# A hybrid decoder layer on one core: the down-projection as seven block products, with sums of its weights made under the up-projection and sums of h kept in DRAM

## The chip, the core and the metric

The kernel runs on one core of a Trainium2 chip. Five engines work side by side, each through its own queue in order: TensorE (PE; its weight loads, PEld, run beside its matmuls), VectorE (DVE), ScalarE (ACT), GpSimd (POOL) and SyncE (SP), which here only starts transfers. ACT starts some transfers too. Tiles lie in SBUF (128 partitions), matmul results in eight PSUM banks of 128x512 float32, which only DVE and ACT read here. Tensors in DRAM are reached by DMA. The metric is the device time of one execution in microseconds (us).

## The reference

One decoder layer over 2048 rows of width 1024, all in float32. The part that matters is the second half of the layer and the final norm:

```python
h = rms_norm(x, g_mlp[l]) * (1.0 + scale_m) + shift_m
u = causal_depthwise_conv(h @ w_up[l], conv_w[l], conv_b[l])
u_gate, u_val = jnp.split(u, 2, axis=-1)
x = x + gate_m * ((jax.nn.silu(u_gate) * u_val) @ w_down[l])
return rms_norm(x, g_final)
```

h is 2048x1024, w_up 1024x5504, w_down 2752x1024. In front of it stand the adaLN vectors, one input projection, two kinds of attention (16 heads) and the output projection.

## The kernel before

**Precision.** An operand x is split into hi and lo of a reduced float32 format: ACT copies x to hi, DVE or POOL subtracts hi from x to get lo (`split`, lines 43 to 45). A product is hi\*hi + hi\*lo + lo\*hi, three matmuls.

**Order.** The program is written as Python loops; a scheduler places each instruction in its engine's queue by an estimated time, within what the buffers allow (`bufs=` is the number of copies of a tile, and a new use waits for the last reader of the old one). Queues then run strictly in order.

**Output projection.** Eight groups of 256 rows (u = 0 to 7). `out_proj` multiplies `mix` by `wo` (L629), adds x (L633) and stores x1 to `x1s`. `finish_out` norms the rows, transposes them in eight pieces on TensorE (L713), lets ACT apply scale and shift into `hf_m` (L715, two buffers), and stores them from ACT's queue to `hm`, one tensor for each of eight pieces kt of h's width and each half (1024 rows) of the rows.

**Up-projection.** For each half `sblk` of the rows and each ci of 21 column blocks, a gate block and a value block of 128 columns are made together. They are treated as a 2x2 block product (halves of the rows, halves of h's width, gate and value) by seven products in place of eight. The seven weight operands come from two loads `wuraw` (512 KB each, three buffers, L781), POOL's sums `ws` and `wuraw` (L796 to L802) and `split` (`wu`, seven buffers). The seven operands of h, `oa` and `ob`, are made once per half by `h_operands` in four steps j: load a piece `xh`, form sums on POOL and DVE, split them. `pair_first` runs the first pair with all seven banks open, j outermost, since the operands arrive by j; `pair` runs the others one product of 12 matmuls after another (L810), reading banks in between (L851 to L866). `conv_tile` and L898 to L901 make the convolution, SiLU and product and store g to DRAM. A last narrow block of 64 gate and 64 value columns ends each half.

**Down-projection.** For each tb of four blocks of 512 rows, 22 pieces k of 128 rows of w_down (the last has 64): load `wdraw` and `graw`, split both, and run 3 matmuls (L960) into each of eight banks (4 row groups t, 2 column halves n). The last four k are held back and run bank by bank, so that L983 to L993 (times gate_m, plus x1, norm, store) overlap them. w_down is loaded and split four times.

Of the kernel before, what the change touches and what calls it, by code (L numbers as in the profile page):

```python
# [1 line left out]

# [31 lines left out]
def kernel(ctx: ExitStack, tc: tile.TileContext, x, c, w_ada, b_ada, g_attn, w_in, b_fgate,  # L34
# [17 lines left out]
    hms = [[dram.tile([P, 2 * TB], F32, name=f"hm{s}_{k}") for k in range(KT)] for s in range(2)]  # L52
# [10 lines left out]
    gate_m = dram.tile([P, D], F32, name="gate_m")  # L63

# [638 lines left out]
    NU = S // HT  # L703

    def finish_out(u, xts):
        sl = slice(u % 4 * HT, (u % 4 + 1) * HT)
# [3 lines left out]
        for kt in range(KT):  # L710
# [6 lines left out]
            nc.scalar.dma_start(hms[u // 4][kt][:, sl], hf)  # L717
# [3 lines left out]

    mixes = {}
    for u in range(NU):
# [10 lines left out]
        finish_out(u, xts)  # L734
    close_pool("p2b", "p2a")
# [3 lines left out]
    NK = KT // 2  # L739
    SB = 2 * TB  # L740
# [9 lines left out]
    def h_operands(sblk, j):  # L750

        pool = ho if j == 0 else ho1
        xh = ho.tile([P, 2, SB], F32, name="xh", bufs=2)
        for i in range(2):
            nc.sync.dma_start(xh[:, i], hms[sblk][j + i * NK])
        b = pool.tile([P, 3, 2, TB], F32R, name=f"ob{j}")
        a = pool.tile([P, 4, 2, TB], F32R, name=f"oa{j}")
        tt = ho.tile([P, 2, TB], F32, name="tt", bufs=1)
        t4 = wp.tile([P, TB], F32, name="t4", tag="ws", bufs=3)
        b11, b12 = xh[:, 0, 0:TB], xh[:, 0, TB:SB]  # L760
        b21, b22 = xh[:, 1, 0:TB], xh[:, 1, TB:SB]

        def put(hi, lo, s, lo_engine=None):
            split(hi, lo, s, lo_engine or nc.vector)

        nc.gpsimd.tensor_sub(tt[:, 0], b22, b12)
        nc.gpsimd.tensor_sub(b12, b12, b11)
        nc.vector.tensor_sub(tt[:, 1], b22, b12)
        nc.vector.tensor_sub(t4, b21, tt[:, 1])
        put(b[:, 0:2, 0], b[:, 0:2, 1], tt)  # L770
        put(b[:, 2, 0], b[:, 2, 1], t4)
        put(a[:, 0, 0], a[:, 0, 1], b11)
        put(a[:, 1:3, 0], a[:, 1:3, 1], xh[:, 1].rearrange("p (a n) -> p a n", n=TB), nc.gpsimd)
        put(a[:, 3, 0], a[:, 3, 1], b12)
        return [a[:, 0], b[:, 1], a[:, 1], a[:, 3], b[:, 0], a[:, 2], b[:, 2]], a
# [32 lines left out]
    def product(b, w, o, j, first, last):  # L808
        for i, (p, q) in enumerate(((0, 0), (0, 1), (1, 0))):
            nc.tensor.matmul(b, w[:, p, j], o[:, q], start=first and i == 0, stop=last and i == 2,  # L810
                             skip_group_check=True)

    def snap():
        return up_.tile([P, TB], F32, name="snap", bufs=4)
# [6 lines left out]
    def pair_first(ws, yg, yv):  # L821
# [17 lines left out]
    def pair(ws, nxt, yg, yv):  # L839

        def run(b, s, first):
            for j in range(NK):
                product(b, ws[s], obs[j][0][s], j, first and j == 0, j == NK - 1)
# [38 lines left out]
    halo = up_.tile([P, 2 * NFULL + 1, 2], F32, name="halo")  # L882
    for sblk in range(2):
        gen = w_operands(0)
        ws = []
        for j in range(NK):
            obs[j] = h_operands(sblk, j)
            ws.extend(next(gen) for _ in range(2 if j < 3 else 1))
        for ci in range(NFULL):
            nxt = w_operands(ci + 1) if ci + 1 < NFULL else None  # L890
# [10 lines left out]
            nc.sync.dma_start(gs[ci][sblk], ug)  # L901
# [4 lines left out]
        oa = [obs[j][1] for j in range(NK)]  # L906
        for j in range(NK):
            product(a, w1, oa[j][:, 0], j, j == 0, j == NK - 1)
# [112 lines left out]
```

## Time and profile before

| what | us |
|---|---|
| three runs, median (lowest to highest) | 3140.04 (3135.02 to 3141.05) |
| the profiled execution | 3137.58 |
| its span, first to last instruction | 3135.8 |
| PE busy in the span | 2962.9 (94%) |
| DVE, ACT, POOL busy | 2142.5, 1650.2, 1281.3 |
| first and last matmul of the up-projection (L810) | 1776.2 and 2644.0 |
| first matmul of the down-projection (L960) | 2653.1 |

Times within the profile count from the start of the span. "Busy" is the time in which an engine executes; matmuls are pipelined, so a row of x44 matmuls is read by where it and the next row start. A duration of one DVE or POOL instruction includes what it waits for once begun. In lists of instructions the columns are start, duration, engine, line, operation, written tile <- read tiles, shape, count, and in brackets the idle time before and what ended it. In the table of stages each engine's busy time is followed by its count of instructions, then come the granted TensorE clock (1.00 is full), the mean busy share of the DMA engines and what they moved.

### The profile page before, as it was taken

What the parts mean: (1) busy time and instruction counts of PE and PEld (TensorE: products, weight loads), DVE (VectorE), ACT (ScalarE), POOL (GpSimd) and SP (SyncE); (2) the same over time, 40 slices, a digit from 0 to 9 for tenths busy, and PEclk for the clock granted to TensorE, in tenths of its full rate; (3) what the DMA queues carried; (4) which work ended last, traced back from release to release, by engine and by line L of the source; (5) the groups of instructions that cost most, each with busy time, mean ns of one, the idle gap of its engine ahead of it and who ended that gap; (6) DMA issues with size and microseconds to landing.
All of it is one profiled execution on the core that took longest, in us unless ns stands there. A gap on an engine that the chain in (4) does not pass through costs nothing. (4 is left out here: it accounts for less than half of the span.)

```text
span 3135.8 us, 46430 instructions
## 1 busy us (share of the span) xinstructions
PE 2962.9 (94%) x15934; PEld 2508.4 (80%) x15934; DVE 2142.5 (68%) x3334; ACT 1650.2 (53%) x3033; POOL 1281.3 (41%) x1523
## 2 busy tenths in 40 slices
PE   6889998999989999999999899999899998999998
PEld 5778787878878888888877688888678887888887
DVE  6787988888866765557832677778887776254253
ACT  5665666666656665567733444444444444333332
POOL 2564455456553343352212444444544442332321
PEclk8999999999999999999999999999999999999999
DMA  9447642556346796595456532223222223554552
GB/s 268 170 149 250 175 139 64 189 178 167 124 150 184 258 279 209 152 328 137 161 186 220 195 98 81 81 81 88 77 89 86 81 81 137 186 199 161 188 200 89
DMA packets 292940, 496.51 MB, mean 158 GB/s; under 512 B 29448, under 2 KB 177664, under 8 KB 291680
## 3 DMA queue, kind: packets, MB, share of 16 engines
q1 hardware_dynamic: 281072, 480.92, 48.0%
q10 hardware_dynamic: 11632, 12.63, 1.1%
q8 instruction: 126, 2.06, 0.3%
q14 instruction: 110, 0.90, 0.1%
HBM read 352.61 MB, written 90.51 MB: 141 GB/s over the span
## 5 line engine op out<-in xcount | busy, mean ns | idle before, releaser
L810 PE MATMUL ps_o<-oa,wu 128*128 128x512 f32 x2088 | 506.2, 393 | 18.1 <-DVE oa L45 12.0
L810 PEld LDWEIGHTS ps_o<-oa,wu 128*128 128x128 f32 x2088 | 392.4, 189 | 110.0 <-DVE oa L45 15.7
L397 PE MATMUL ps_pv<-at,V 128*128 128x256 f32 x2304 | 404.7, 294 | 36.2 <-DVE at L393 19.5
L393 DVE TENSOR_TENSOR at<-ps_pt,at 128x512 fp32r<-128x512 f32 (+1 forms) x576 | 364.0, 652 | 107.2 <-ACT at L392 104.2
L281 PE MATMUL ps_pj<-hp,w_qk 128*128 128x512 f32 x1512 | 415.2, 405 | 14.2 <-DMA hp<-hs 4.4
L392 ACT ACTIVATE at<-ps_pt 128x512 fp32r<-128x512 f32 (+1 forms) x576 | 314.4, 576 | 210.2 <-PE ps_pt L388 161.0
L420 POOL TENSOR_TENSOR a<-a,r 128x512 f32<-128x512 f32 (+3 forms) x240 | 286.8, 1196 | 309.8 <-DVE r L419 88.5
L397 PEld LDWEIGHTS ps_pv<-at,V 128*128 128x128 f32 x2304 | 334.6, 191 | 81.0 <-DVE at L393 34.5
L281 PEld LDWEIGHTS ps_pj<-hp,w_qk 128*128 128x128 f32 x1512 | 275.6, 191 | 68.7 <-DMA hp<-hs 6.9
L45 DVE TENSOR_TENSOR wd<-wdraw,wd 128x1024 fp32r<-128x1024 f32 x88 | 111.8, 1271 | 263.0 <-ACT wd L44 262.9
L45 POOL TENSOR_TENSOR g<-graw,g 128x512 fp32r<-128x512 f32 x84 | 142.3, 1696 | 326.5 <-ACT g L44 325.8
L378 PE MATMUL ps_qk<-K,Q 128*128 128x512 f32 (+2 forms) x640 | 265.7, 417 | 9.6 <-DMA K<-q 5.6
L419 DVE TENSOR_TENSOR_SCAN r<-r 128x513 f32<-128x513 f32 x192 | 258.9, 1360 | 19.4 <-ACT r L410 11.5
L960 PE MATMUL ps_o<-wd,g 128*128 128x512 f32 x1040 | 251.1, 391 | 8.7 <-ACT g L44 8.7
L810 PE MATMUL ps_t<-ob,wu 128*128 128x512 f32 x984 | 242.5, 391 | 0.3 <-ACT wu L44 0.3
L379 PE MATMUL ps_qk<-K,Q 128*128 128x512 f32 (+2 forms) x640 | 237.8, 373 | 0.0
L320 PE MATMUL ps_pj<-w_v,hp 128*128 128x256 f32 (+1 forms) x1536 | 230.8, 290 | 6.6 <-DVE q L290 2.9
L960 PEld LDWEIGHTS ps_o<-wd,g 128*128 128x128 f32 x1040 | 196.2, 189 | 50.0 <-ACT g L44 9.2
L44 ACT ACTIVATE wu<-wuraw 128x512 fp32r<-128x512 f32 x214 | 133.1, 626 | 184.2 <-PE ps_o L810 111.8
L320 PEld LDWEIGHTS ps_pj<-w_v,hp 128*128 128x128 f32 x1536 | 210.1, 193 | 16.5 <-DVE q L290 3.8
L810 PEld LDWEIGHTS ps_t<-ob,wu 128*128 128x128 f32 x984 | 185.3, 189 | 39.8 <-ACT wu L44 0.7
L44 ACT ACTIVATE wd<-wdraw 128x1024 fp32r<-128x1024 f32 x88 | 93.1, 1058 | 213.3 <-PE ps_bc L960 197.9
(218 smaller groups left out, 5834.1 us busy)
## 6 DMA issues: line engine op xcount, KB each, us to landing
hp<-hs SPq DMA_DIRECT2D x224, 512.0 KB
wuraw<-in_w_up_dram SPq DMA_DIRECT2D x84, 512.0 KB
wdraw<-in_w_down_dram SPq DMA_DIRECT2D x84, 512.0 KB
Q<-q SPq DMA_DIRECT2D x128, 256.0 KB
g<-u SPq DMA_DIRECT2D x42, 512.0 KB
graw<-g SPq DMA_DIRECT2D x84, 256.0 KB
hs<-hp SPq DMA_DIRECT2D x32, 512.0 KB
K<-q SPq DMA_DIRECT2D x128, 128.0 KB
```

The source lines that it names most:

```text
L45: (lo_engine or nc.gpsimd).tensor_sub(lo, src, f(hi))
L281: nc.tensor.matmul(acc, w[kt][:, a, n], h[:, bb], start=kt == 0 and i == 0, stop=kt == KT - 1 and i == 2)
L320: nc.tensor.matmul(av[:, t * width:(t + 1) * width], hts[kt][:, a, tok], w[1][kt][:, bb, 0:width], start=kt == 0 and m == 0, stop=kt == KT ...
L378: nc.tensor.matmul(b[:, :cw], Q[:, hl, 0, qcols], K[:, hl, :cw], start=True, stop=False)
L379: nc.tensor.matmul(b[:, :cw], Q[:, hl, 1, qcols], K[:, hl, :cw], start=False, stop=True)
L392: nc.scalar.activation(at[:, 0, lo:], b[:, lo:], AF.Copy)
L393: nc.vector.tensor_sub(at[:, 1, lo:], b[:, lo:], f(at[:, 0, lo:]))
L397: nc.tensor.matmul(o[:, 0:2 * P], V[kt // 4][:, kt % 4, hl, :], rhs, start=first and kk == 0 and w == 0, stop=last and kk == 1 and w == 1)
L419: nc.vector.tensor_tensor_scan(rev, rev, rev, 1.0, ALU.mult, ALU.bypass)
L420: (nc.vector if (ch + qi) % 4 == 0 else nc.gpsimd).tensor_mul(a[:, :need], a[:, :need], r[:, 1:need + 1])
L810: nc.tensor.matmul(b, w[:, p, j], o[:, q], start=first and i == 0, stop=last and i == 2, skip_group_check=True)
L960: nc.tensor.matmul(banks[t][n], g[:, a, t * P:(t + 1) * P], w[:, b, n * TB:(n + 1) * TB], start=k == 0 and i == 0, stop=k == NKD - 1 and i ...
```

## The change

**The down-projection** becomes the seven-product scheme as well: pairs m of 128-row pieces of w_down (11 pairs, the last padded with zeros), halves of the output columns, and pairs of 128-row groups of g. Work goes in three chunks of pairs (3, 4, 4), and in each over eight row groups tp of 256 rows: 63 or 84 matmuls per unit (now L1041). The seven weight operands `wb` (from `wbraw`, three buffers) are made once per chunk and stay; the seven operands of g, `ga`, are made for each unit from `graw`. Results are added to x1 (`xo`), which is stored to `x1s` between chunks and normed in the last.

**Sums of w_down**, times gate_m, are made on POOL under the up-projection (`down_sums`, `mix_sums`) and stored to `wds`. One step of it, or of `h_sums` for the second half, is traced behind each store of g: 16 steps with POOL work in the first half, 10 in the second.

**Operands of h** are stored by operand (`hmo`). `h_sums(0)` loads, mixes on POOL and stores the sums during the last four groups of the output projection, `h_sums(1)` under the first half. `h_operand` then loads a whole operand (1 MB) and splits it, and the opening pair runs product after product.

**Buffers:** `wu` nine for seven, `snap` three for four; the last stores of g go to ACT's queue; the first weights of the second half are made at the end of the first.

```diff
+    def mix_sums(x):
+        q11, q12, q21, q22 = x
+        nc.gpsimd.tensor_sub(q22, q22, q12)
+        nc.gpsimd.tensor_sub(q12, q12, q11)
+        nc.gpsimd.tensor_add(q11, q22, q11)
+        nc.gpsimd.tensor_sub(q21, q21, q11)
+
+    def h_sums(sblk):
+        for j in range(NK):
+            x = square_tile()
+            q = [x[:, i, n * TB:(n + 1) * TB] for i in range(2) for n in range(2)]
+            for part, o in zip(q, (0, B12, 2, 5)):
+                nc.sync.dma_start(part, hmo[sblk][o][:, j])
+            mix_sums(q)
+            for part, o in ((q[3], 4), (q[1], 3), (q[0], 1), (q[2], 6)):
+                nc.sync.dma_start(hmo[sblk][o][:, j], part)
+            yield
...
         finish_out(u, xts)
+        if u >= NU // 2:
+            next(sums)
...
+    ORDER = (1, 4, 6, 0, 3, 2, 5)
+    def h_operand(sblk, o):
+        raw = square_tile().rearrange("p a (b n) -> p (a b) n", n=TB)
+        nc.sync.dma_start(raw, hmo[sblk][o])
+        b = (ho if o in ORDER[:1] else ho1).tile([P, 2, NK, TB], F32R, name=f"ob{o}")
+        split(b[:, 0], b[:, 1], raw, nc.gpsimd if o in ORDER[-2:] else nc.vector)
+        return b
+
+    def down_sums(ms):
+        gt = ho.tile([P, D], F32, name="gt", bufs=1)
+        nc.sync.dma_start(gt, gate_m)
+        yield
+        for m in ms:
...
+            for i, rows_ in ((0, P), (1, n)):
+                row = (2 * m + i) * P
+                nc.sync.dma_start(x[0:rows_, i], w_down[row:row + rows_, :])
+                nc.gpsimd.tensor_mul(x[:, i], x[:, i], gt)
+            a1, a2, b1, b2 = (x[:, i, n * TB:(n + 1) * TB] for i in range(2) for n in range(2))
+            yield
+            for o, part in ((0, a1), (2, b1), (5, b2)):
+                nc.sync.dma_start(to[o], part)
+            mix_sums((a1, a2, b1, b2))
+            for o, part in ((4, b2), (3, a2), (1, a1), (6, b1)):
+                nc.sync.dma_start(to[o], part)
+            yield
...
-        w = wp.tile([P, 2, NK, P], F32R, name="wu", bufs=7)
+        w = wp.tile([P, 2, NK, P], F32R, name="wu", bufs=9)
...
-        for j in range(NK):
-            for s in (1, 4, 6, 0, 2, 5, 3):
-                product(banks[s], ws[s], obs[j][0][s], j, j == 0, j == NK - 1)
+        for s in ORDER:
+            for j in range(NK):
+                product(banks[s], ws[s], obs[s], j, j == 0, j == NK - 1)
...
+            stored = nc.sync.dma_start(gs[ci][sblk], ug)
+            if ci >= 3 * sblk:
+                with tc.issue_after(stored.ins):
+                    next(side, None)
...
+    def down_operand(c, o):
+        n = CHUNKS[c][1]
+        w = dw.tile([P, 2, 4, TB], F32R, name="wb", bufs=7)
+        raw = wr.tile([P, 4, TB], F32, name="wbraw", bufs=3)
+        nc.sync.dma_start(raw[:, 0:n], wds[c][o])
+        split(w[:, 0, 0:n], w[:, 1, 0:n], raw[:, 0:n], nc.gpsimd if o > 4 else nc.vector)
+        return w
+
+    def g_operands(c, tp):
...
+        nc.gpsimd.tensor_sub(s3, a11, a21)
+        nc.gpsimd.tensor_add(a21, a21, a22)
+        nc.gpsimd.tensor_sub(s2, a21, a11)
+        yield put(a11)
+        yield put(s2)
+        yield put(a12)
+        nc.gpsimd.tensor_sub(a12, a12, s2)
+        yield put(a21)
+        yield put(s3, nc.gpsimd)
+        yield put(a12, nc.gpsimd)
+        yield put(a22, nc.gpsimd)
...
+        def run(b, o, first, last):
+            for m in range(n):
+                for k, (p, q) in enumerate(((0, 0), (0, 1), (1, 0))):
+                    nc.tensor.matmul(b, ga[o][:, p, m], wbs[o][:, q, m], start=first and m == 0 and k == 0,
+                                     stop=last and m == n - 1 and k == 2, skip_group_check=True)
+            if nxt is not None:
+                later.append(next(nxt))
+            if turn:
+                wlater.append(down_operand(c + 1, o))
```

**How the queues move.** First TensorE's queue where the up-projection opens. x are rows being transposed, ob and oa operands of h, ps_o, ps_t and ps_bc the banks. Before:

```order
L713 MATMUL ps_t<-edge,x_21652 128x128
L810 MATMUL ps_o<-oa_21867,wu 128x512 x2
L713 MATMUL ps_t<-edge,x_21597 128x128
L713 MATMUL ps_t<-edge,x_21652 128x128
L810 MATMUL ps_bc<-ob_21839,wu 128x512 x2
L810 MATMUL ps_o<-oa_21867,wu 128x512 x2
```

And now (the 12 matmuls of ob_21878, the first operand, stand among the last transposes of group u = 6; all 16 transposes of group u = 7 follow in one block, which ends in the first two rows):

```order
L721 MATMUL ps_t<-edge,x_21657 128x128
L721 MATMUL ps_t<-edge,x_21712 128x128
L850 MATMUL ps_t<-ob_21883,wu 128x512
L850 MATMUL ps_bc<-ob_21888,wu 128x512
L850 MATMUL ps_t<-ob_21883,wu 128x512 x11
L850 MATMUL ps_bc<-ob_21888,wu 128x512 x11
L850 MATMUL ps_o<-ob_21893,wu 128x512 x12
```

Transposes that were strewn between products now stand in front of all products but the first.

Then POOL's queue in one pair of the steady up-projection (xh holds the side work, gt is gate_m; y and halo belong to the convolution). Before:

```order
L796 TENSOR_TENSOR ws<-wuraw 128x512
L797 TENSOR_TENSOR wuraw<-wuraw 128x512
L874 COPY halo<-y 128x2
L798 TENSOR_TENSOR ws<-wuraw 128x512
L873 MEMSET y 128x2
L802 TENSOR_TENSOR wuraw<-wuraw,ws 128x512
```

And now:

```order
L736 TENSOR_TENSOR xh<-xh 128x512
L737 TENSOR_TENSOR xh<-xh 128x512
L836 TENSOR_TENSOR ws<-wuraw 128x512
L738 TENSOR_TENSOR xh<-xh 128x512
L914 COPY halo<-y 128x2
L837 TENSOR_TENSOR wuraw<-wuraw 128x512
L739 TENSOR_TENSOR xh<-xh 128x512
L838 TENSOR_TENSOR ws<-wuraw 128x512
L913 MEMSET y 128x2
L842 TENSOR_TENSOR wuraw<-wuraw,ws 128x512
```

POOL's four sums for the next weights now alternate with four sums of the side work; in every other pair two `L807 TENSOR_TENSOR xh<-xh,gt 128x1024` stand there instead.

Last, SP's queue over the same stretch. Before:

```order
L901 DMA g_0_164<-u 128x1024
L781 DMA wuraw<-in_w_up_dram 128x8x128 x2
L901 DMA g_0_166<-u 128x1024
L781 DMA wuraw<-in_w_up_dram 128x8x128 x2
L901 DMA g_0_168<-u 128x1024
```

And now:

```order
L946 DMA g_0_156<-u 128x1024
L811 DMA wd_0_235<-xh 128x512
L811 DMA wd_0_237<-xh 128x512
L811 DMA wd_0_240<-xh 128x512
L821 DMA wuraw<-in_w_up_dram 128x8x128 x2
L814 DMA wd_0_239<-xh 128x512
L814 DMA wd_0_238<-xh 128x512
L814 DMA wd_0_236<-xh 128x512
L814 DMA wd_0_241<-xh 128x512
L946 DMA g_0_158<-u 128x1024
L806 DMA xh<-in_w_down_dram 128x1024 x2
```

The loads of the next weights now stand behind stores that wait for POOL, and the store of g behind four more.

More of the change, by code (lines that the diff above doesn't have):

```diff
@@ L1 @@
 from contextlib import ExitStack
+from itertools import chain
 import concourse.bass as bass
@@ L748 @@
     obs = {}
[L750 to L775, printed above, removed]
@@ L809, in product @@
         for i, (p, q) in enumerate(((0, 0), (0, 1), (1, 0))):
-            nc.tensor.matmul(b, w[:, p, j], o[:, q], start=first and i == 0, stop=last and i == 2,
+            nc.tensor.matmul(b, w[:, p, j], o[:, q, j], start=first and i == 0, stop=last and i == 2,
                              skip_group_check=True)
     def snap():
-        return up_.tile([P, TB], F32, name="snap", bufs=4)
+        return up_.tile([P, TB], F32, name="snap", bufs=3)
     def y_tile():
@@ new lines @@
+        b = bank_a()
+        run(b, 1, True, True)
+        take(1, L, b)
+        run(a, 2, False, True)
+        take(0, L, a)
+        square(0, L)
+        run(b, 3, False, True)
+        take(1, H, b)
+        d = bank_c()
+        run(d, 4, True, True)
+        take(1, H, d)
+        square(1, H)
+        run(b, 5, False, True)
+        take(0, H, b)
+        square(0, H)
+        norm(0)
+        run(d, 6, False, True)
+        take(1, L, d)
+        square(1, L)
+        norm(1)
+        ga = later
```

181 lines of the change are left out of this document (102 added, 79 removed).

## The prediction

> **What bounds the kernel now.** I read the span by stages first (busy time per engine in stretches cut where the work changes), then the pitch of the matmuls, the waits of TensorE, and the places where DVE and POOL run together.
>
> ```profile
> core 0: us, PE busy (x) PEld busy (x) DVE busy (x) ACT busy (x) POOL busy (x), PEclk, DMA share, GB/s
> 1600.00:1776.00 176.00, 163.27 (x747) 130.24 (x746) 64.07 (x112) 70.78 (x150) 51.66 (x60) 0.98 0.68 221
> 1776.00:1812.00 36.00, 27.82 (x108) 20.28 (x107) 28.43 (x26) 20.89 (x36) 23.43 (x13) 0.86 0.43 146
> 1812.00:2205.00 393.00, 391.58 (x1716) 320.72 (x1715) 312.71 (x354) 176.63 (x249) 167.85 (x168) 1.00 0.27 82
> 2205.00:2252.00 47.00, 33.94 (x116) 24.08 (x115) 43.51 (x40) 21.29 (x30) 27.22 (x16) 0.85 0.28 84
> 2252.00:2644.30 392.30, 389.98 (x1710) 319.89 (x1710) 303.12 (x346) 171.80 (x241) 162.75 (x117) 1.00 0.26 78
> 2644.30:2653.10 8.80, 0.09 (x1) 0.00 (x0) 5.00 (x5) 3.87 (x4) 0.00 (x0) 0.77 1.00 344
> 2653.10:3127.80 474.70, 474.67 (x2080) 392.41 (x2080) 186.80 (x214) 165.31 (x252) 142.29 (x84) 0.99 0.53 177
> 3127.80:3135.80 8.00, 0.00 (x0) 0.00 (x0) 3.50 (x7) 1.02 (x3) 0.00 (x0) 0.66 0.35 131
> ```
>
> The rows are, in order: output projection; opening of the first half of the up-projection; its steady part; opening of the second half; steady part; gap; down-projection; tail. TensorE is full in three of them, 1260 us together. The openings, the gap and the tail are where it stands still.
>
> ```profile
> 3107.46 9.93 PEld L960 LDWEIGHTS ps_o<-wd,g 128*128 128x128 f32 x44
> 3117.43 4.95 PEld L960 LDWEIGHTS ps_t<-wd,g 128*128 128x128 f32 x22
> ```
>
> 44 weight loads, each with its matmul, take 3117.43 - 3107.46 = 9.97 us: a pitch of 0.2266 us. 2080 of them are 471.3 us, so the down-projection is a chain of matmuls with nothing to gain but their number. A pair of column blocks in the up-projection is 7 x 12 matmuls, 19.04 us. By this pitch the openings lose 36 - 86 x 0.2266 - 2 (20 transposes) = 14.5 us and 47 - 116 x 0.2266 = 20.7 us; 86 and 116 are the rows' counts without the transposes.
>
> **The matmuls removed.** Before, 21 blocks x 3 products x 8 banks and 16 more, four times: 2080. After, 7 products x 3 x 11 row pairs x 8 row groups: 1848, of the same form. 232 x 0.2266 = **-52.6 us**, if TensorE stays the bound.
>
> **Start of the down-projection.** It opens late now:
>
> ```profile
> 2653.12 2.07 PE L960 MATMUL ps_o<-wd,g 128*128 128x512 f32 x4 [8.73 <-ACT g L44]
> 2651.49 1.06 ACT L44 ACTIVATE wd<-wdraw 128x1024 fp32r<-128x1024 f32 x1 [1.26 <-DMA wdraw<-in_w_down_dram]
> 2652.58 1.23 DVE L45 TENSOR_TENSOR wd<-wdraw,wd 128x1024 fp32r<-128x1024 f32 x1 [1.10 <-ACT wd L44]
> ```
>
> After, the seven weight operands are 128x1536: by these rows some 1.5 us of ACT and 1.8 us of DVE each. The loads of three stand in SP's queue ahead of the last stores of g, the other four wait for a raw buffer and for 4 MB of g and x1 ahead of them, 12 us at the gap's 344 GB/s. Between 0 (all hidden, as two row groups share each operand) and 22 us (four operands one after the other: 2.3 us of load at 344 GB/s, 3.3 of splitting); I take **+9**, nearer the low end.
>
> **Two changes of row chunk.** Each brings 7 x 1 MB, 7 ACT copies near 2 us, 5 DVE subtractions near 2.3 and 2 on POOL near 4.6 (twice the 1024 rows here and below), into a unit of 63 x 0.2266 = 14.3 or 84 x 0.2266 = 19 us; a buffer is free only when its old product is done. Three raw buffers hold the first three, so 4 MB are not prefetched, 12 us of DMA beside the unit's own 3 MB. 0 to 15 us each; I take 4 each, since every operand has a whole unit until it is used: **+8**. Banks read between products (a window of 9 to 12 matmuls): 0 to 10, **+4**. Tail: one POOL product of 1.3 us takes the place of a 0.7 us DVE one, **+1**. The 48 loads and 32 stores of x1 are 42 MB; with them the stage moves some 93 MB in 430 us, 216 GB/s, below 344: nothing.
>
> **The sums of h ahead of the up-projection.** 16 POOL operations and 32 transfers (8.4 MB, 24 us at 344 GB/s) enter the output projection, whose DMA share is 0.68. SP's stores now wait for POOL, and the loads of o and r that feed the next mix queue behind them. TensorE stands still 176 - 163.27 = 13 us there as it is, and the mixes are made one row group ahead, which hides a late load of a few us. Between -2 (two of the four column pieces of h are no longer prepared there) and +12 (the idle time nearly doubled); **+4**. Without that row group ahead, each late mix would hold TensorE.
>
> **First opening.** The order put all transposes of the last 256 rows in one block, ahead of the second product. Each pair of them waits for its buffers to be stored:
>
> ```profile
> 1787.93 1.06 ACT L44 ACTIVATE ob<-tt 128x1024 fp32r<-128x1024 f32 x1 [2.70 <-DVE tt L768]
> 1791.34 1.00 ACT L715 ACTIVATE hf_m<-ps_t,mod_m 128x256 f32<-128x256 f32 x2
> 1803.74 1.00 ACT L715 ACTIVATE hf_m<-ps_t,mod_m 128x256 f32<-128x256 f32 x2
> ```
>
> Between these rows lie three pairs: (1803.74 - 1791.34) / 3 = 4.1 us, and two more stand between them at 1794.69 and 1798.60, so 3.4 at best. Six pairs follow the last output matmul: 20 to 25 us with 12 products (2.7 us) in them. ACT splits the second operand only behind them; the others come at load (about 5 us), copy (2), subtraction (2.3), with two raw buffers. TensorE fills some of it with the next pair's products. I get a loss of 24 us for 14.5: **+10** (0 to +20). **Second opening.** The first two sums are loaded under the last pairs, the others through the same two buffers during the 11 us of the last narrow block, and the first weights of this half are split under the end of the other: I put the loss at 7 us for 20.7, **-14** (-18 to 0).
>
> **POOL's work under the up-projection.** This is the term that can turn the sum. 26 pairs get 4 subtractions 128x512 or 2 products 128x1024 more.
>
> ```profile
> 1744.53 1.29 POOL L766 TENSOR_TENSOR tt<-xh 128x512 f32<-128x512 f32 x1 [6.06 <-DMA xh<-hm]
> 1745.78 2.38 POOL L45 TENSOR_TENSOR oa<-xh,oa 128x1024 fp32r<-128x1024 f32 x1
> 2409.60 1.40 POOL L796 TENSOR_TENSOR ws<-wuraw 128x512 f32<-128x512 f32 x1 [7.09 <-DMA wuraw<-in_w_up_dram]
> 2411.08 2.16 POOL L797 TENSOR_TENSOR wuraw<-wuraw 128x512 f32<-128x512 f32 x1
> 2409.17 0.68 DVE L45 TENSOR_TENSOR wu<-wuraw,wu 128x512 fp32r<-128x512 f32 x1
> 2409.77 2.32 DVE L879 SCALAR_TENSOR_TENSOR u<-y,conv,u 128x1024 f32<-128x1024 f32 x1
> 2399.48 1.28 DVE L879 SCALAR_TENSOR_TENSOR u<-y,conv,u 128x1024 f32<-128x1024 f32 x1
> 2402.39 1.21 DVE L900 TENSOR_TENSOR u<-u 128x1024 f32<-128x1024 f32 x1
> ```
>
> Alone, DVE's L879 takes 1.28 us. Begun at 2409.77 under POOL's L796 (to 2411.00) it takes 2.32, as if it began near 2410.8; POOL's next, begun at 2411.08, takes 2.16 for 1.29, as if it began near 2411.95, just before DVE's end at 2412.09. They take turns. A pair has 7 x 0.68 + 4 x 1.28 + 1.21 = 11.1 us of such DVE work and 4 x 1.29 = 5.2 of POOL's; with 5.0 more it is 21.3 us against 19.04. But an end overlaps the next beginning by 0.18 (POOL) and 0.14 us (DVE); taking that off 8 and 12 operations leaves 18.2. So it just fits, or just doesn't.
>
> The Trainium skill, "SBUF — State Buffer", section "Who interferes with whom", says the same of these two engines: a DVE instruction with two SBUF inputs and a GpSimd one that reads SBUF exclude each other for the whole instruction. Held strictly it gives the 21.3; the trace agrees with the turns, and its overlaps with a little less than the strict sum.
>
> ```profile
> L45 DVE TENSOR_TENSOR wu<-wuraw,wu 128x512 fp32r<-128x512 f32 x102 | 86.1, 845 | 7.0 <-ACT wu L44 7.0
> L879 DVE SCALAR_TENSOR_TENSOR u<-y,conv,u 128x1024 f32<-128x1024 f32 x40 | 61.4, 1537 | 0.0
> L878 DVE SCALAR_TENSOR_TENSOR u<-y,conv,u 128x1024 f32<-128x1024 f32 x41 | 59.6, 1455 | 14.1 <-ACT u L876 14.1
> PEld ps_o L810 <- DVE snap L859: 5.1, 11, 0.8
> PEld ps_o L810 <- ACT wu L44: 2.4, 1, 2.4
> ```
>
> All but the last row are of the first steady part (20.6 pairs), the last of the second. DVE waited 102 x 0.165 + 40 x 0.257 + 41 x 0.175 = 34 us, 1.7 a pair, for 4 POOL operations. Twice as many make it 3.4, and DVE's 312.7 / 20.6 = 15.2 us a pair become 16.9 of 19.04. TensorE waited 5.1 us for DVE to read a bank, 0.25 a pair; fuller, I take 0.4 more, 26 x 0.4 = 10, less 3 as two more weight buffers spare waits like the last row: **+7** (-5 to +55). Three snap buffers for four cost nothing: each comes back two products, 5.4 us, before its next use. Behind a late DVE stands everything: bank reads, weight splits, then SP's weight loads.
>
> **Sum:** -52.6 + 9 + 8 + 4 + 1 + 4 + 10 - 14 + 7 = -23.6 us. The profiled execution is 3137.58 (span 3135.8 and 1.8 around it): 3114.0. The median of the runs, 3140.04, lies 2.5 above it: **3116 us**.
>
> **Rivals.** (1) Slower: DVE and POOL, not TensorE, set the pace of the up-projection. At 21.3 us the 26 pairs cost 26 x 2.2 = 57 instead of 7: 3166. It decides from a pair of 19.04 + (23.6 + 7) / 26 = 20.2 us on. For it: DVE is busy 80% already, in a fixed order. Against it: the overlaps, and DVE's idle time before weight splits. 0.18. (2) No change: the gain is given back where operands are remade; a start of +18 and chunk changes of +10 each instead of 9 and 4 add 21: 3137. For it: DMA at 344 GB/s is full in the gap. Against it: three raw buffers. 0.15. (3) The joins hide: chunk changes, bank reads, output projection and first opening cost nothing and the weight buffers bring 3, so 8 + 4 + 4 + 10 + 10 less: 3080. 0.17. My forecast has the other 0.50; its own range is 3095 to 3133.
>
> **Numbers.** About 0.2% (6 us) can be told from no change. Faster: 0.49 of mine, 0.17 of (3), 0.03 of (2): 0.69. Same: 0.01, 0.09 of (2), 0.01 of (1): 0.11. Slower: 0.17 of (1), 0.03 of (2): 0.20. From 3076 to 3166 half of (3)'s lower part and half of (1)'s upper part fall out, under 0.2.
>
> **What would show it.** Down-projection between first and last matmul near 440 us with 1848 matmuls; pairs with side work at 19.0 to 19.5 us, DVE near 90% there; the opening near 2205 shortened to about 35 us, the first one lengthened to about 45. Pairs above 20.2 us, or TensorE waiting for wb and ga all through the last stage, would make it wrong.

## The result, and the profile after

| | old kernel | changed kernel |
|---|---|---|
| median of the runs | 3140.55 us (4 runs, 3135.02 to 3141.38) | 3231.72 us (4 runs, 3228.10 to 3236.41) |
| profiled execution, its span | 3137.58, 3135.8 us | 3232.28, 3230.5 us |

The ratio is 1.0295, with an interval of 1.0277 to 1.0313: the change makes the kernel 2.95% slower, where 0.8% faster was predicted. The time lies 66 us above 3166, the top of the widest range given, and 99 us above 3133, the top of the forecast's own. The prediction's sign of being wrong, pairs above 20.2 us, came too: they take 21.9 and 21.1 us in the mean.

The stretches of the changed kernel first (us from the span's start and length, then busy time and instructions of TensorE, weight loads, DVE, ACT and POOL, the granted clock, the DMA share and GB/s). They are cut at events: first and last matmul of a stage, and, inside the up-projection, ACT's first copy of a bank in the third pair and in the last one, so that the two long rows hold 18 pairs each.

```profile
1598.10:1798.80 200.70, 175.88 (x777) 138.92 (x777) 65.36 (x115) 69.69 (x151) 72.82 (x76) 0.94 0.72 235
1798.80:1804.80 6.00, 0.71 (x3) 0.29 (x3) 0.71 (x2) 2.47 (x2) 0.00 (x0) 0.70 0.90 354
1804.80:1873.70 68.90, 53.71 (x201) 39.55 (x202) 39.20 (x36) 33.31 (x42) 18.42 (x15) 0.80 0.39 130
1873.70:2267.30 393.60, 362.73 (x1511) 288.06 (x1511) 302.44 (x306) 151.25 (x216) 247.76 (x196) 0.97 0.46 143
2267.30:2346.60 79.30, 73.04 (x311) 58.85 (x310) 69.62 (x66) 42.14 (x49) 39.48 (x27) 0.98 0.46 141
2346.60:2726.50 379.90, 352.44 (x1499) 282.76 (x1498) 289.61 (x305) 150.56 (x216) 201.21 (x139) 0.98 0.37 112
2726.50:2755.90 29.40, 29.40 (x130) 24.02 (x128) 17.14 (x19) 10.22 (x12) 5.42 (x6) 1.00 0.47 170
2755.90:2765.30 9.40, 0.01 (x1) 0.00 (x0) 8.40 (x10) 6.10 (x9) 1.50 (x2) 0.74 0.39 133
2765.30:3222.70 457.40, 435.51 (x1848) 354.29 (x1848) 308.74 (x368) 174.95 (x300) 279.24 (x191) 0.96 0.57 194
```

The old kernel cut at the same events:

```profile
1590.40:1776.20 185.80, 173.07 (x782) 138.07 (x783) 67.60 (x121) 74.98 (x159) 53.64 (x62) 0.97 0.69 224
1776.20:1831.50 55.30, 46.80 (x191) 35.63 (x189) 46.43 (x46) 30.24 (x49) 33.08 (x24) 0.91 0.35 113
1831.50:2176.30 344.80, 344.09 (x1509) 282.13 (x1508) 268.78 (x307) 152.65 (x218) 145.22 (x144) 1.00 0.28 83
2176.30:2264.40 88.10, 74.64 (x294) 57.43 (x293) 81.83 (x81) 41.40 (x57) 44.34 (x30) 0.92 0.28 87
2264.40:2612.90 348.50, 346.18 (x1518) 283.98 (x1518) 268.52 (x308) 154.91 (x222) 157.31 (x113) 1.00 0.27 82
2612.90:2644.40 31.50, 31.49 (x139) 25.64 (x137) 22.20 (x25) 11.20 (x14) 1.29 (x2) 1.00 0.09 34
```

Row against row, and with the down-projection's 474.7 us and the gap's 8.7:

| part | predicted us | measured us |
|---|---|---|
| POOL's side work under the up-projection (the two rows of 18 pairs) | +7 | +48.8 and +31.4, **+80.2** |
| output projection (to its last matmul) | +4 | **+14.9** |
| first opening (6.0 + 68.9 for 55.3) | +10 | **+19.6** |
| second opening (79.3 for 88.1) | -14 | -8.8 |
| end of the up-projection (29.4 for 31.5) | 0 | -2.1 |
| start and length of the down-projection (9.4 + 457.4 for 8.7 + 474.7) | -52.6 + 9 + 8 + 4 = -31.6 | **-16.6** |
| tail | +1 | -0.2 |
| before the output projection's second row group, where no line was changed | 0 | +7.7 |
| sum | -23.6 | +94.7 |

The last row but one is scatter: the first matmul of L635 starts between 1513 and 1523 us in the kernels of the experiments below, all with the same code ahead of it.

**How a pair became 22 us long.** One pair with side work in the changed kernel, POOL's and DVE's rows of L918 and L919 in order of time (start, length, engine, line, tile, and in brackets the idle time before it and what ended it):

```profile
2009.41 1.29 POOL L736 TENSOR_TENSOR xh<-xh 128x512 f32<-128x512 f32 x1 [2.72 <-DMA wd<-xh]
2009.42 2.36 DVE L918 SCALAR_TENSOR_TENSOR u<-y,conv,u 128x1024 f32<-128x1024 f32 x1 [0.57 <-ACT u L916]
2010.78 2.15 POOL L737 TENSOR_TENSOR xh<-xh 128x512 f32<-128x512 f32 x1
2012.31 1.71 DVE L919 SCALAR_TENSOR_TENSOR u<-y,conv,u 128x1024 f32<-128x1024 f32 x1
2012.90 2.27 POOL L836 TENSOR_TENSOR ws<-wuraw 128x512 f32<-128x512 f32 x1
2013.94 2.32 DVE L918 SCALAR_TENSOR_TENSOR u<-y,conv,u 128x1024 f32<-128x1024 f32 x1
2015.14 2.26 POOL L738 TENSOR_TENSOR xh<-xh 128x512 f32<-128x512 f32 x1
2016.29 2.19 DVE L919 SCALAR_TENSOR_TENSOR u<-y,conv,u 128x1024 f32<-128x1024 f32 x1
2018.49 1.28 POOL L837 TENSOR_TENSOR wuraw<-wuraw 128x512 f32<-128x512 f32 x1
2019.72 1.29 POOL L739 TENSOR_TENSOR xh<-xh 128x512 f32<-128x512 f32 x1
2020.97 1.26 POOL L838 TENSOR_TENSOR ws<-wuraw 128x512 f32<-128x512 f32 x1
2022.26 0.63 ACT L45 ACTIVATE wu<-ws 128x512 fp32r<-128x512 f32 x1 [7.15 <-POOL y L913]
2022.94 7.12 PE L850 MATMUL ps_o<-ob,wu 128*128 128x512 f32 x23 [2.24 <-ACT wu L45]
```

While both engines run, POOL's 1.29 us become 2.15 to 2.27 and DVE's 1.28 become 1.7 to 2.4: each waits for the other, operation by operation. L738 and L739 and the weight sums L836 to L838 of the next pair stand mixed in POOL's order. L838, the sum that the next pair's second product needs, ends at 2022.2; ACT copies it at once, and TensorE has been waiting 2.24 us. The waits of TensorE over the first 18 pairs (total, times, longest):

```profile
PE ps_o L850 <- ACT wu L45: 16.6, 9, 3.9
PE ps_o L850 <- DVE snap L899: 10.1, 10, 2.5
```

DVE's groups of instructions over the same pairs (shapes and count, then busy time, mean ns of one, idle time before):

```profile
L918 DVE SCALAR_TENSOR_TENSOR u<-y,conv,u 128x1024 f32<-128x1024 f32 x36 | 70.6, 1962 | 13.1 <-ACT u L916 13.1
L919 DVE SCALAR_TENSOR_TENSOR u<-y,conv,u 128x1024 f32<-128x1024 f32 x36 | 65.3, 1813 | 0.4
...
L895 DVE TENSOR_TENSOR snap<-ps_o,snap 128x512 f32<-128x512 f32 x18 | 12.3, 684 | 0.9
```

L918, whose tensors all lie in SBUF, takes 1.96 us in the mean; L895, which reads one bank of PSUM, keeps its 0.68 us.

**And the clock fell.** The same wait with the matmuls around it, as stretches (columns as above):

```profile
2008.00:2020.70 12.70, 12.70 (x57) 10.17 (x55) 9.78 (x7) 3.94 (x4) 11.21 (x7) 1.00 0.50 150
2020.70:2023.00 2.30, 0.06 (x2) 0.06 (x1) 0.08 (x1) 0.74 (x2) 1.57 (x3) 1.00 0.31 114
2023.00:2026.50 3.50, 3.50 (x9) 2.60 (x10) 3.50 (x5) 1.45 (x3) 2.13 (x2) 0.51 0.09 36
2026.50:2029.00 2.50, 2.50 (x13) 2.03 (x12) 2.50 (x5) 2.28 (x4) 0.60 (x2) 1.00 1.01 352
```

After 2.24 us without a matmul the granted clock is one half for 3.4 us: 9 matmuls in 3.5 us, where 0.2266 us each would let 15 through. So the wait cost some 1.5 us more. In the first row of 18 pairs the clock is 0.97 in the mean, and 0.03 x 393.6 = 11.8 us go that way, beside 393.6 - 362.73 = 30.9 us of standing still (0.7 before); in the second 0.02 x 379.9 = 7.6 beside 27.5 (2.3 before). Some 7 of the first row's 48.8 us are in neither; they lie in TensorE's busy time and stay unexplained.

### The profile page after: what moved, and what is told of

Same layout as the page of the kernel before. It is cut to its first block, busy times and chain, and to the rows that moved or that the text cites. A ratio compares the mean times of both kernels' runs of the same rounds, so it can differ in the third digit from the quotient of the medians.

```text
span 3230.5 us, 46837 instructions
## 1 busy us (share of the span) xinstructions
PE 2961.0 (92%) x15702; PEld 2486.7 (77%) x15702; DVE 2295.0 (71%) x3451; ACT 1658.2 (51%) x3060; POOL 1573.0 (49%) x1716
## 3 DMA queue, kind: packets, MB, share of 16 engines
q1 hardware_dynamic: 315712, 542.28, 52.6%
## 4 chain that ended last, share of the span: by engine, by line
PE 16%; DVE 9%; DMA 9%; POOL 7%; issue 5%; ACT 2%; SPq 2%; POOLq 0%; ACTq 0%; DVEq 0%
PE ps_o L850 6%; PE ps_o L1041 5%; PE ps_t L1041 2%; DVE wu L46 2%; PE ps_t L850 2%; DMA r<-rstd 2%; DVE u L918 1%; DMA hm<-hf_m 1%; POOL ws L838 1%; DMA xh<-in_w_down_dram 1%; DVE u L919 1%; POOL wuraw L837 1%; DMA xh<-hm 1%; POOL xh L807 1%; DMA wd<-xh 1%
## 5 line engine op out<-in xcount | busy, mean ns | idle before, releaser
L850 PE MATMUL ps_o<-ob,wu 128*128 128x512 f32 x2592 | 642.7, 401 | 60.7 <-ACT wu L45 32.2
L850 PEld LDWEIGHTS ps_o<-ob,wu 128*128 128x128 f32 x2592 | 494.8, 193 | 189.6 <-ACT wu L45 38.5
L403 PE MATMUL ps_pv<-at,V 128*128 128x256 f32 x2304 | 405.1, 294 | 37.0 <-DVE at L399 20.1
L1041 PE MATMUL ps_o<-wb,ga 128*128 128x512 f32 x1320 | 320.3, 398 | 21.8 <-DVE xo L1049 11.1
L287 PEld LDWEIGHTS ps_pj<-hp,w_qk 128*128 128x128 f32 x1512 | 276.5, 192 | 70.3 <-DMA hp<-hs 8.8
L1041 PEld LDWEIGHTS ps_o<-wb,ga 128*128 128x128 f32 x1320 | 252.7, 192 | 79.7 <-DVE xo L1049 13.6
L850 PE MATMUL ps_t<-ob,wu 128*128 128x512 f32 x1008 | 254.4, 394 | 11.9 <-ACT ob L45 8.3
L394 PE MATMUL ps_pt<-edge,a 128*128 128x128 f32 x1088 | 184.6, 279 | 18.8 <-POOL a L426 11.2
L416 ACT ACTIVATE r<-ps_qk 128x512 f32<-128x512 f32 (+2 forms) x320 | 173.1, 541 | 52.8 <-PE ps_qk L385 47.7
L46 DVE TENSOR_TENSOR wu<-wuraw,wu 128x512 fp32r<-128x512 f32 x214 | 181.9, 867 | 11.5 <-ACT wu L45 11.1
L916 ACT ACTIVATE u<-y,conv 128x1024 f32<-128x1024 f32 x86 | 106.8, 1244 | 149.1 <-DVE y L906 82.3
```

Of the source, the lines that this page charges most:

```text
L46: (lo_engine or nc.gpsimd).tensor_sub(lo, src, f(hi))
L287: nc.tensor.matmul(acc, w[kt][:, a, n], h[:, bb], start=kt == 0 and i == 0, stop=kt == KT - 1 and i == 2)
L403: nc.tensor.matmul(o[:, 0:2 * P], V[kt // 4][:, kt % 4, hl, :], rhs, start=first and kk == 0 and w == 0, stop=last and kk == 1 and w == 1)
L850: nc.tensor.matmul(b, w[:, p, j], o[:, q, j], start=first and i == 0, stop=last and i == 2, skip_group_check=True)
L1041: nc.tensor.matmul(b, ga[o][:, p, m], wbs[o][:, q, m], start=first and m == 0 and k == 0, stop=last and m == n - 1 and k == 2, skip_group_ ...
```

## The experiments

Each was run once with a profile unless it says otherwise, so a few us between two of them say nothing (the changed kernel's own four runs span 8.3 us); the old kernel took 3142.83 us beside e1 to e8, 3144.25 beside e9, 3142.69 beside e10 and e11. The table gives, from cuts at the same events as above, the mean pair in the two rows of 18 pairs (side arithmetic comes with 16 and 10 pairs of the two halves, with 12 and 10 in e8 and e11, with 33 in all in e9), the output projection from its first matmul at L635 to its last, and the down-projection from its first to its last.

| kernel | total us | first half's pairs | second half's pairs | output projection | down-projection |
|---|---|---|---|---|---|
| old (profiled run) | 3137.58 | 19.2 | 19.4 | 264.3 | 474.7 |
| changed (profiled run) | 3232.28 | 21.9 | 21.1 | 278.9 | 457.4 |
| e1 no side arithmetic | 3169.01 | 19.6 | 19.6 | 276.1 | 457.8 |
| e2 writes instead | 3178.76 | 20.2 | 19.8 | 278.9 | 462.8 |
| e3 weights first | 3247.87 | 22.4 | 21.3 | 277.7 | 461.2 |
| e4 stores on POOL's queue | 3230.26 | 22.2 | 21.1 | 277.0 | 456.2 |
| e5 side work on DVE | 3185.34 | 20.5 | 20.1 | 278.4 | 456.6 |
| e6 less POOL | 3163.58 | 20.5 | 20.1 | 277.1 | 441.9 |
| e7 no sums of h | 3241.41 | 22.0 | 21.3 | 276.5 | 470.1 |
| e8 sums at load | 3184.83 | 21.1 | 21.4 | 265.5 | 439.6 |
| e9 spread | 3205.78 | 20.7 | 21.6 | 266.8 | 449.9 |
| e10 POOL's queue for h | 3236.17 | 22.0 | 21.2 | 280.6 | 461.7 |
| e11 nine buffers | 3181.47 | 20.7 | 20.7 | 265.3 | 444.9 |
| e12 e6 once more (profiled run) | 3168.63 | 20.5 | 20.0 | 279.7 | 442.7 |

**e1: the side arithmetic left out.**

```diff
-                nc.gpsimd.tensor_mul(x[:, i], x[:, i], gt)
...
-            mix_sums((a1, a2, b1, b2))
...
-            mix_sums(q)
+            if sblk == 0:
+                mix_sums(q)
```

> The products with the gate and the eight sums of a row pair, and the sums of the second half of h, are left out under the up-projection; their loads and stores stay, 26 pairs with them as before. Three theories of why a pair with side work takes 22 us instead of 19.1. Turns: POOL and DVE exclude each other operation by operation, and 21.3 us of such work do not fit in a pair. Order: the side work stands ahead of the next pair's weight sums, in POOL's order and in SP's queue, and the operands come late. Traffic: the added loads and stores. Turns and order both expect pairs of 19.1 to 19.5 us here, the up-projection at 870 to 880 us instead of 951, about 3155 us in all. Traffic expects 22 us pairs still and 3220 to 3232.

Measured 3169.01 us, pairs of 19.6 us, just above the 19.1 to 19.5 of turns and order. Traffic as the cause of the 22 us falls. But 8.4 and 3.4 us over the old kernel's rows stay when of the side work only the loads and stores are left (the number of weight buffers and h by operand differ from the old kernel here too), and the total lies 14 us above the 3155.

**e2: as much POOL time, but nothing read.**

```diff
-                nc.gpsimd.tensor_mul(x[:, i], x[:, i], gt)
+                nc.gpsimd.memset(x[:, i], 0.0)
+                nc.gpsimd.memset(x[:, i], 0.0)
+                nc.gpsimd.memset(x[:, i, 0:TB], 0.0)
...
+        for q in (q22, q12, q11, q21):
+            nc.gpsimd.memset(q, 0.0)
+            nc.gpsimd.memset(q, 0.0)
+            nc.gpsimd.memset(q[:, 0:TB // 2], 0.0)
```

> Every side product and sum of the up-projection is replaced by writes of zeros on POOL into the same place that take about as long together (2.4 us for a product of 1024 columns, 1.3 for a sum of 512), with the same loads and stores; the sums are left out. These writes read nothing. Turns expects that they do not hold DVE up: pairs of 19.1 to 19.8 us, 3155 to 3175 in all. Order expects that the time alone counts, since they stand at the same place in POOL's order: pairs of 21 to 22 us, 3210 to 3232.

Measured 3178.76 us: 4 above the range of the turns and 31 below that of the order; the first half's 20.2 us a pair also lie above the 19.8 of the turns, and below 21. Its first stretch of 18 pairs:

```profile
1868.20:2231.50 363.30, 347.61 (x1508) 281.00 (x1507) 260.27 (x306) 150.61 (x217) 200.36 (x299) 1.00 0.50 156
```

In it, the group of writes of 512 columns on POOL, those of DVE that are L918 and L919 in the changed kernel, and last the old kernel's group that became L918:

```profile
L745 POOL MEMSET xh<- 128x512 f32 x40 | 21.0, 526 | 11.7 <-DMA wd<-xh 5.7 <-DMA xh<-hm 3.1 <-issue 2.8
...
L929 DVE SCALAR_TENSOR_TENSOR u<-y,conv,u 128x1024 f32<-128x1024 f32 x36 | 53.9, 1498 | 0.1
L928 DVE SCALAR_TENSOR_TENSOR u<-y,conv,u 128x1024 f32<-128x1024 f32 x36 | 52.4, 1456 | 13.2 <-ACT u L926 13.1
...
L878 DVE SCALAR_TENSOR_TENSOR u<-y,conv,u 128x1024 f32<-128x1024 f32 x36 | 51.0, 1417 | 13.2 <-ACT u L876 13.2
```

POOL is busy 200 us in 363, and DVE's operation takes 1.46 us instead of 1.96 (1.42 in the old kernel): the time on POOL is there, the reading is not, and the clock stays at 1.00. That the writes come in shorter pieces than the sums isn't the reason: from 1868 to 2667 us, 27 operations of L928 and L929 ran beside such writes and no other work of POOL, and took 1.28 us, as long as the 55 during which POOL was idle (1.27). The Trainium skill, "SBUF — State Buffer", section "Who interferes with whom", states just this difference: a DVE instruction with two SBUF inputs contends with a GpSimd one that reads SBUF, not with one that only writes. Of the 80.2 us that the two rows gained, 11.8 stay in e1 with the transfers alone, e2 has another 14.6 with POOL's time as such (18.5 and 7.9 us in its two rows, 26.4 in all), and 53.8 are there only when the side work reads.

**e3: the weight sums ahead of the side work.**

```diff
+            if stored is not None and s == 0:
+                with tc.issue_after(stored.ins), tc.issue_after(sums_done[-1].ins):
+                    next(side, None)
...
-            if ci >= 3 * sblk:
-                with tc.issue_after(stored.ins):
-                    next(side, None)
+            stores.append(stored)
```

> Nothing is left out. Each side step is issued two pairs later, behind the three sums of the next pair's weights, so that on POOL the weight sums come first and on SP their loads are ahead of the side stores. Order expects pairs of 19.2 to 19.9 us and 3155 to 3180 in all. Turns expects that the same work has to be done in the same pairs: 21.5 to 22.2 us, 3215 to 3235.

`sums_done[-1]` is the sum s2 of the next pair's weights, `stored` the store of g two pairs back. Measured 3247.87 us, slower than the changed kernel and above both ranges. The weights now come in time, and the wait has moved; TensorE's waits in its first 18 pairs:

```profile
PE ps_o L852 <- DVE snap L904: 22.2, 10, 5.0
PE ps_o L852 <- DVE snap L900: 18.3, 9, 3.3
```

DVE's reads of the banks are late now, 40.5 us instead of 10.1 + 1.4, and the clock is 0.96. Order alone isn't the cause; what is held up is both engines, and order only chooses which of them TensorE waits for.

**e4: the stores on POOL's queue.** In `down_sums` the two `nc.sync.dma_start(to[o], part)` become `nc.gpsimd.dma_start(to[o], part)`.

> Nothing is left out. The seven stores of each row pair's sums are issued from POOL's queue instead of SP's, so that no load of weights waits behind a store that waits for POOL. If SP's queue is what makes the operands late: pairs of 19.5 to 20.5 us where row pairs are summed, 3165 to 3195 in all. If it is the turns, or POOL's order alone: 21.5 us or more, 3215 to 3245.

3230.26 us and 22.2 us a pair in the first half, 21.1 in the second: the places of these stores in SP's queue aren't what holds the weights up. The transfers of h's sums stayed on SP, but the second half has none.

**e5: the side work on DVE.** `mix_sums` under the up-projection and the product with `gt` on `nc.vector`.

> Nothing is left out. The side products and sums of the up-projection run on DVE (0.68 us for a sum of 512 columns) instead of POOL (1.29). If a POOL operation shuts DVE out for its whole length, the work that takes turns shrinks from 21.3 to about 18.8 us of a 19.04 us pair, and DVE itself is busy some 18 us: pairs of 19.5 to 20.3 us instead of 22.1, 3170 to 3195 in all. If DVE's fullness is the trouble and not the turns, it gets worse: pairs of 22.5 us or more, over 3240.

3185.34 us, 46 less, by giving DVE more to do. Its first stretch of 18 pairs:

```profile
1868.70:2238.60 369.90, 353.42 (x1522) 284.33 (x1521) 289.79 (x359) 151.64 (x218) 117.21 (x144) 1.00 0.48 154
```

And the group of the products there:

```profile
L807 DVE TENSOR_TENSOR xh<-xh,gt 128x1024 f32<-128x1024 f32 x12 | 15.5, 1294 | 4.2 <-DMA xh<-in_w_down_dram 4.1
```

DVE does 53 operations more than in the changed kernel (359 to 306) in less busy time, 289.8 us for 302.4. The product takes 1.29 us on DVE and took 2.4 alone on POOL. The total is as expected, the pairs are slower than the 19.5 to 20.3 us expected: those with side work still take 20 to 21.6 us in the main. TensorE waits 16.0 us in 15 waits for DVE's L895 in this stretch, and 0.5 us for anything else. DVE is the slow one now.

**e6: less POOL in the other stages too.** As e5, the sums of the first half of h on DVE as well, and in the down-projection:

```diff
-        split(w[:, 0, 0:n], w[:, 1, 0:n], raw[:, 0:n], nc.gpsimd if o > 4 else nc.vector)
+        if o > 4:
+            nc.scalar.activation(w[:, 0, 0:n], raw[:, 0:n], AF.Copy)
+            for m in range(n):
+                nc.gpsimd.tensor_sub(w[:, 1, m], raw[:, m], f(w[:, 0, m]))
...
-        yield put(s3, nc.gpsimd)
+        yield put(s3)
```

(and so for `a12` and `a22`).

> Nothing is left out. As the kernel before in this list, and also: the sums of the first half of h under the output projection on DVE; in the down-projection all weight-side and row-side splits of 128x512 on DVE, and POOL's subtractions of 128x2048 cut into four. If the turns cost the down-projection its waits too (TensorE waited 11.1 us for DVE's L1049 and 10.0 for late copies of wb there): 440 to 450 us instead of 457 from its first matmul to its last, and the output projection 5 to 15 us shorter. If the loads and the change of row chunk set these waits: 455 to 460, and the output projection as long as it was (279).

The kernel before it in that list is e5. 3163.58 us; the down-projection takes 441.9 us, as the turns would have it, the output projection 277.1 as ever, against the 5 to 15 us less that they would have brought there. What one long subtraction on POOL does in the changed kernel's down-projection:

```profile
2917.69 4.62 POOL L46 TENSOR_TENSOR wb<-wbraw,wb 128x2048 fp32r<-128x2048 f32 x1
2918.36 4.50 DVE L46 TENSOR_TENSOR ga<-graw,ga 128x512 fp32r<-128x512 f32 x1 [0.16 <-DMA wbraw<-wd]
```

A subtraction of 0.68 us on DVE lasts 4.50 and ends 0.55 us after POOL's. In e6 that stage has POOL busy 190.7 us instead of 279.2. The two edits to this stage were made together; which of them brings more was not tried.

**e7: the sums of the first half of h left out, e10: their transfers on POOL's queue.** In `h_sums`, `if sblk:` ahead of `mix_sums(q)`; and `(nc.sync if sblk else nc.gpsimd).dma_start` for its loads and stores.

> The sixteen subtractions and additions of the sums of the first half of h, on POOL under the output projection, are left out; their loads and stores stay. If POOL's arithmetic (its turns with DVE, and SP's stores that wait for it) made the output projection 14.7 us longer: it takes 264 to 268 us again from its first matmul to its last, and 3215 to 3222 in all. If it is the traffic and the places in SP's queue: 276 to 279, and 3228 to 3234.

> Nothing is left out. The 32 loads and stores of the sums of the first half of h go through POOL's queue instead of SP's; the sums stay. If their places in SP's queue (stores that wait for POOL ahead of the loads of o, r and x) made the output projection longer: 264 to 269 us from its first matmul to its last. If it is the traffic itself, which makes the stores of hf_m land late: 275 to 280. The up-projection as before, so 3215 to 3235 in all.

The output projection takes 276.5 and 280.6 us, not 264 to 269: so neither the arithmetic nor the places in SP's queue explain its length. The totals (3241.41, 3236.17) lie somewhat above what was expected; the down-projection took 470.1 and 461.7 us in them with no line of it changed, so this stage scatters by 10 us and more between kernels. What is left is the traffic, and e8, which changes more than that, agrees.

**e8: the operands of h made at load, as in the old kernel.** `hms`, `h_operands`, the narrow block and seven weight buffers of the old kernel; down-projection as in e6; `down_sums` on DVE.

> Nothing is left out. The operands of h are made at load as in the old kernel (no sums of h through DRAM, seven weight buffers), the down-projection has its seven products with the changes of the kernel e6, and the products and sums of the down weights run on DVE under the up-projection, 22 steps. By the turns: up-projection 868 + 22 x 0.8 = 886, output projection as in the old kernel (264), down-projection 445 to 457: 3125 to 3150 in all, near the old kernel's 3140. If the sums through DRAM are not what made the output projection and the first opening longer: 3160 to 3180.

3184.83 us, above both ranges. Where the sums don't go through DRAM, the output projection takes 265.5 us and the first opening 54.1 (old kernel: 264.3 and 55.2): both terms are gone. ACT's waits for stores of hf_m to land there, in the changed kernel and in the old one (total, times, longest):

```profile
ACT hf_m L723 <- DMA hm<-hf_m: 31.8, 12, 5.9
ACT hf_m L715 <- DMA hm<-hf_m: 8.6, 6, 3.8
```

This is one way in which the traffic may reach TensorE, and it wasn't tried by itself. It can be a part only: TensorE's own waits for hf_m rise from 8.2 to 13.0 us there, those for DVE's x (L639 and L717, L633 and L709 before) from 2.6 to 12.1. The pairs with side work fall back to 22 us in the mean here, which took the gain away.

**e11: nine weight buffers for seven, e9: side work spread over three steps.** Both as e8, `wu` with 9 and `snap` with 3 buffers and the smaller operand of h's first row pair made only behind the output projection (for its place). e9 also makes the second half's first weights ahead, and steps `x[:, 0]` by `gt`, `x[:, 1]` by `gt` and the sums in three pairs, each behind DVE's L942.

> Nothing is left out. As e8, with nine weight buffers and three snap buffers, and the smaller operand of h's first row pair made only when the output projection has ended. If the number of weight buffers was why the pairs of e8 (22.2 us with side work) were slower than those of e5 (20.7): pairs of 20.5 to 21 us, the up-projection at 900 to 910 us instead of 938, 3145 to 3160 in all. If it is the order of the side work: 22 us still, 3175 to 3190.

> Nothing is left out. As e8, with nine weight buffers and three snap buffers (as in the changed kernel), the weights of the second half's first pair made ahead (as there), and the side work of a row pair in three steps instead of two, each behind DVE's last product of a pair: 35 pairs with 1.3 to 2.7 us more on DVE instead of 22 with 2.5 to 2.7. If it is DVE's time and the turns that set the pace: pairs of 19.2 to 20 us, the up-projection at 870 to 885 us, 3105 to 3130 in all, below both kernels. If each step with its transfers costs a pair 1.5 us whatever it holds: 35 x 1.5 = 52 us, and 3150 to 3165.

In e11 the pairs with side work take 20 to 21.3 us in the main, the mean of all is 20.7: the number of buffers was most of the difference between e8 and e5. Its total, 3181.47 us, misses: the late operand leaves a hole of 15.6 us ahead of the up-projection, and the gap ahead of the down-projection is 17.1 us. e9 misses by more, 3205.78 us: many of its pairs take 19.1 us and others 22 to 25, with TensorE waiting for DVE's reads of banks (27.4 us at L903 and 17.5 at L899 over the up-projection). Why isn't shown: of 26 such waits over 0.7 us, only in 10 is an operation of the side work among the five ahead of the read in DVE's order; in the others they are weight splits, bank reads and the convolution.

**e12: e6 once more, timed.**

> The kernel e6 once more, timed against the old kernel in three rounds: is what the moved side work and the cut splits bring (3163.6 in one run) steady, and does it reach the old kernel? If the two effects are real: 3158 to 3168, ratio 1.005 to 1.009, between the two kernels. If the one run was a lucky one: 3175 or more.

As expected of a steady effect: 3167.02 us (4 runs, 3164.21 to 3169.72) against 3146.87 for the old kernel (7 runs): a ratio of 1.0068, interval 1.0049 to 1.0086. It takes back 2% of the changed kernel's time and isn't faster than the old one. No kernel here is.

## Why the prediction was wrong

**The step that failed** is the one on POOL's work under the up-projection: the overlaps taken off the strict sum, "leaves 18.2. So it just fits, or just doesn't", and then, for TensorE's wait in a pair, "I take 0.4 more". The turns themselves were read rightly, and so was DVE's load: 16.9 us a pair predicted, 302.44 / 18 = 16.8 measured. What the step left out is the other side. POOL too is held up: it is busy 247.76 / 18 = 13.8 us a pair, where the same operations alone (1.29 us a sum, 2.4 a product) would take some 10.2, and the weight sums stand in the middle of that. In the old kernel it was 145.22 / 18 = 8.1 for some 5.7. Two engines with spare time of their own still deliver late when each works in a fixed order and waits for the other. I asked whether the sum of the busy times fits into a pair, and took the answer for the wait of TensorE, from 0.25 us a pair to 0.65. It is 1.7 (30.9 / 18), and with the slower clock 2.4 ((30.9 + 11.8) / 18).

**The rival** that POOL and DVE set the pace had the right mechanism, shown by e1, e2 and e5 together, and too low a price: 21.3 us a pair as the strict sum, where pairs with side work take some 22. It had no term for the transfers (11.8 us in e1), nor for the clock after a wait (11.8 + 7.6 us by the rows' clock). The clock of 0.85 in the openings, which the prediction quoted, was a sign of it. The Trainium skill, "TensorE: Matmul & The Clock Gate", section "HAM oscillation — how this bites in real kernels", gives about 3.4 us without a matmul as the limit; here 2.24 us were followed by half the clock, so the measurement, which decides, is stricter than the page.

**Down-projection.** 52.6 us for 232 matmuls of the same pitch were right as arithmetic, and "near 440" came true where the splits were cut and moved: 441.9 in e6, 439.6 in e8, 444.9 in e11, 442.7 in e12; 449.9 in e9. The eight kernels without that edit took 456.2 to 470.1. In the changed kernel it was 457.4, with TensorE waiting for L1049 and for copies and subtractions of wb:

```profile
PE ps_o L1041 <- DVE xo L1049: 11.1, 6, 3.8
PE ps_o L1041 <- ACT wb L45: 10.0, 2, 9.4
PE ps_t L1041 <- DVE wb L46: 6.4, 2, 5.2
```

The term that was mis-sized is that of chunk changes and bank reads, +8 and +4. It counted "2 on POOL near 4.6" as durations, not as 4.6 us in which DVE stands still; the edits of e6 brought 15.5 us. That is not the whole of it, since in e6 TensorE's waits for L1049 (there L1054) and for ACT's copies of wb stay:

```profile
PE ps_o L1046 <- DVE xo L1054: 12.0, 8, 3.3
PE ps_o L1046 <- ACT wb L45: 11.8, 2, 11.3
```

Its 441.9 us are still 23.1 more than 1848 x 0.2266. The start, +9, was too much: the gap grew by 0.7. So rival (2), that the gain is given back where operands are remade, came true in part, by 15 us (-16.6 for -31.6), and in the chunks rather than at the start; of rival (3) none of the joins hid, neither these nor the output projection nor the first opening.

**Sums of h ahead of the up-projection** were +4 (up to +12) and measured 14.9, outside the bounds. The mechanism named, SP's stores waiting for POOL with the loads of o and r behind them, falls by e7 and e10; without the sums through DRAM the cost is gone (e8), and how the traffic makes it stays open. The 8.4 MB were taken as 24 us of a stage with room for them; the prediction had the DMA share of 0.68 and didn't ask what late landings do to the stores of hf_m, of which two buffers exist.

**The openings.** The first was +10 (0 to +20) and is +19.6, the upper end. e8 shows that it comes with h by operand; which part of that (the block of transposes, or operands of 1 MB one after the other) stays open. The second was -14 (-18 to 0) and is -8.8. The tail took 0.2 us less where 1 more was predicted. Three snap buffers for four weren't tried by themselves.

## What to carry to other kernels

Where two engines shut each other out, count each operation of one as standing time of the other, in both directions, and follow the one result that the bound engine needs through that order; a sum of busy times below the length of the stage says little. Work for such a pair belongs on the engine that shuts the other out for the shorter time (1.29 us for 2.4 here). Short pieces should let the other in between; they were tried only together with other edits (e6). A bound TensorE can pay for a wait twice, once by standing still and once by its clock.

## What was not expected of the hardware

- After a wait of TensorE of 2.24 us the clock was 0.51 for 3.4 us (rows above). In the changed kernel's up-projection behind its first opening all seven waits over 2.4 us were followed by such a fall. Length alone doesn't decide, though: one of 1.88 us in e5 was followed by a fall, one of 2.18 us in e2 and one of 3.31 us in e8 weren't.
- In each trace the clock changes only at moments whole multiples of 3.41 us apart, and what counts is how long TensorE stands still between two neighbouring ones. From 1860 to 3100 us of the 14 traces, half the clock followed each of the 129 such stretches at full clock with 1.95 us or more of standing still, and 3 of the some 4,700 with less than 1.85; in between some fell. The wait of 2.24 us lay whole in one stretch, the 3.31 us of e8 were split into 1.82 and 1.49.
- POOL writing 512 columns (0.53 us) leaves DVE alone, POOL reading them (1.29 us) doesn't: the same operation on DVE took 1.28 us beside writes alone, and 1.96 us in the mean of the changed kernel.
- More operations on DVE took less of DVE's busy time (e5: 359 in 289.8 us, changed kernel: 306 in 302.4).
